# Product 2 of the gate and up projections by a second Strassen level, and a new order of a pair of tiles

## The chip, the cores and the metric

One NeuronCore of a Trainium2 chip runs the whole program. The metric is the device time of one execution in microseconds (us); lower is better. The engines run side by side, each with a queue of its own in order: TensorE (PE, matmuls), VectorE (DVE), ScalarE (ACT), GpSimdE (POOL) and SyncE (SP, which issues the DMAs).

## What is computed

One inference step of a hybrid decoder layer over 1048 tokens (16 meta tokens, 1024 of the prompt, 8 samples), in float32. Cut to what matters here:

```python
D_MODEL, D_FF = 1024, 2816

def swiglu(x, wg, wu, wd):
    return (jax.nn.silu(x @ wg) * (x @ wu)) @ wd

h = h + 0.5 * swiglu(rmsnorm(h, n1), w1g, w1u, w1d)      # FFN 1
...                                                      # two scans (HGRN2, Mamba-2) and projections
h = h + 0.5 * swiglu(rmsnorm(h, n2), w2g, w2u, w2d)      # FFN 2
```

The change is in the gate and up projections (`x @ wg`, `x @ wu`) of both FFNs.

## The kernel before

**Numbers.** A float32 factor is split into a high part (a cast to the reduced type float32r, on ScalarE) and a low part (the rest, a subtraction on VectorE). A product of two factors is then three matmuls: high-high, high-low, low-high (`mm3`, lines 163 to 165).

**Blocks.** Tokens stand in the free dimension in four quarters of Q columns (262 in FFN 1, which has 1048 tokens, and 258 in FFN 2, where 16 are dropped). The 22 tiles of 128 hidden columns are worked in 11 pairs, `i` = 0 to 10; the tiles of a pair are here called a and b. Gate and up of a tile are one 2 x 2 block product (two weight matrices by two halves of the 1024 inputs; two quarters of tokens), made by Strassen's scheme in its Winograd form: seven products named 1, 5, 6, 7, 2, 3, 4, of four k-tiles each, for each of the two halves c of the tokens. One product for one half is one step of 12 matmuls. `Blocks` makes the token operands, `Left` the weight operands: `load` (DMA on SP), `sum_` (VectorE, line 460), `hi` (ScalarE cast, line 464), `lo` (VectorE, line 468).

**The nested part.** In pairs 3 to 10 product 3 of the two tiles is not done outright: `Inner` treats product 3 of a and of b together as one more 2 x 2 product and does it by seven inner products of two k-tiles and Q columns (6 matmuls each, 42 for what would be 48). `Inner.operands` makes its token operands once in an FFN, `begin` its weight sums and splits, `product` its matmuls, and `post` adds the results to the partial sums x of the two tiles.

**PSUM.** Eight banks: two double banks (pool `acc`, both halves c of one outer product) and four single ones (pool `mis`, the inner products). A double bank is taken when the first matmul into it is issued and comes free when its last reader has run.

**Order.** In the FFNs the order of TensorE, VectorE, ScalarE and SP is written by hand. `Steps` is a list of matmul steps; `before(i, fn)` hangs work ahead of step i, and what is hung there is issued to the other engines' queues in that order, then the step's matmuls, then its `post`. So each engine's queue has a fixed order. A pair before: a's products 1, 6, 2, 5, 7, then b's 1, a's 4, b's 2, 6, 5, 7, inner 1 6 and 5 7, b's 4, inner 2 3 and 4. After product 4 of both, `post` multiplies by the norm factor (`times_r`, line 670), ScalarE applies SiLU, and VectorE multiplies gate by up (`product_`, line 717) into a hidden tile.

**After a pair.** `Hidden.jobs` makes four differences of hidden blocks (line 954), which the down projection's own Strassen products need, into extra tiles, and stores all seven blocks to DRAM (line 957). `down` follows pair 10: its loads, casts (line 979) and lows (line 983) of the first hidden operands, and those of its weights (lines 1040, 1045), begin some steps before the gate and up stage ends.

Fixed pools that matter: 6 weight tiles `ws` (high and low together), 8 raw weight tiles `r`, 9 temporaries `t`, 8 slots `s` and 30 slots `u`.

Of the kernel before, what the change touches and what calls it, by code (L numbers as in the profile page):

```python
# [17 lines left out]
P = 128  # L18
D = 1024
# [423 lines left out]
class Left:  # L443
# [12 lines left out]
    def sum_(self, p):  # L456
        x, y, op = {5: (7, 4, ALU.add), 6: (5, 1, ALU.subtract), 7: (1, 7, ALU.subtract), 3: (2, 6, ALU.subtract)}[p]
        if p not in self.raw:
            self.raw[p] = self.K.raw(self.n * P)
        self.K.nc.vector.tensor_tensor(self.raw[p], self.raw[x], self.raw[y], op)  # L460
# [68 lines left out]
ORDER6 = (1, 6, 2, 5, 7, 4), (1, 2, 6, 5, 7, 4)  # L529


class Inner:
# [4 lines left out]
    def __init__(self, K, ops, op=None):  # L537
        self.K, self.ops = K, ops
        self.op = {} if op is None else op
        self.raw, self.w, self.ps = {}, {}, {}  # L540
        self.then, self.out = {}, {}

    def next(self):
        return Inner(self.K, self.ops, self.op)

    def half(self, c, h):
        n = 2 * self.K.Q
        return tuple(x[:, h * n : h * n + n] for x in self.ops[c].op[3])

    def operands(self):  # L550
# [3 lines left out]
        t = K.slot("u", K.T)  # L554
        a, b, d = t[:, :n], t[:, n : 2 * n], K.slot("s", K.T)[:, :n]
# [23 lines left out]
    def begin(self, S, s0):  # L579

        K, nc = self.K, self.K.nc
        f, g = self.raw.pop(0), self.raw.pop(1)
        tmp = K.slot("u", K.T)
        s = tmp[:, :512]
        self.z, self.v = (tmp[:, 512 + i * K.Q : 512 + i * K.Q + K.Q] for i in range(2))

        def sums():
            nc.vector.tensor_add(s[:, :256], g[:, :256], g[:, 256:])
            nc.vector.tensor_sub(s[:, 256:], s[:, :256], f[:, :256])

        def sum7():
            nc.vector.tensor_sub(g[:, :256], f[:, :256], g[:, :256])

        def sum3():
            nc.vector.tensor_sub(f[:, 256:], f[:, 256:], s[:, 256:])

        def hi(i, src):
            self.w[i] = K.ws()
            nc.scalar.copy(self.w[i][:, : src.shape[1]], src)

        def lo(i, src):
            w = src.shape[1]
            nc.vector.tensor_sub(self.w[i][:, 512 : 512 + w], src, self.w[i][:, :w].bitcast(F32))

        for at, fn, *args in (
            (2, sums), (3, sum7), (5, hi, 0, f), (6, lo, 0, f), (6, sum3), (6, hi, 1, s), (7, lo, 1, s),
            (7, hi, 2, g), (8, lo, 2, g), (9, hi, 3, f[:, 256:]), (10, lo, 3, f[:, 256:]),
        ):
            S.before(s0 + at, lambda fn=fn, args=args: fn(*args))

    def step(self, S, *ps):

        def mm():
            for p in ps:
                self.product(p)
                self.post(p)

        S.add(mm)

    def product(self, p):  # L620
        K = self.K
        b = {2: 1, 3: 5, 4: 7}.get(p, p)
# [3 lines left out]
        i, o = {1: (0, 0), 2: (0, 256), 5: (1, 0), 6: (1, 256), 7: (2, 0), 4: (2, 256), 3: (3, 0)}[p]  # L626
# [6 lines left out]
    def post(self, p):  # L633
        nc = self.K.nc
        add = nc.vector.tensor_add
        z, v, x, y = self.z, self.v, self.out[0](), self.out[1]()
        ps = self.ps[{2: 1, 3: 5, 4: 7}.get(p, p)]
        if p == 1:
            nc.scalar.copy(z, ps)
        elif p == 6:  # L640
            add(v, ps, z)
            add(y, y, v[:, None, :].broadcast_to([P, 2, self.K.Q]))
            add(x[:, 1], x[:, 1], v)
        elif p == 5:
            add(y[:, 1], ps, y[:, 1])
        else:
            t = {7: y[:, 1], 2: x[:, 0], 3: x[:, 1], 4: y[:, 0]}[p]
            add(t, ps, t)


def pair(K, S, wg, wu, f, ops, spread, hid, late_r, first=None, inner=None):
# [21 lines left out]
    def post(p, cs, b):  # L673
# [11 lines left out]
        elif p == 7:  # L685
            nc.vector.tensor_add(temp("u1", cs), b, temp("x", cs))
            if inner:
                times_r("u1", 1, cs)
# [6 lines left out]
        elif inner:  # L695
            t = temp("v", cs)
            nc.vector.tensor_add(t, b, t)
            tm["u0"] = tm["v"]
            times_r("u0", 0, cs)
            product_(0, cs)  # L700
# [17 lines left out]

    if inner:
        i = f % 2  # L720
        left.plan(S, s0, 0, 2 * i, ORDER6[i], ((0, 2, 4, 6, 8, 12), (0, 4, 6, 8, 10, 14))[i])
        unit = Unit(K, left.w, [o.op for o in ops], 4, post)

        def both(*ps):
            for p in ps:
                for c in range(2):
                    unit.step(S, p, c, (0, 1))

        def keep():
            inner.raw[i] = left.raw[3]  # L730

        cs = slice(0, 2)

        def gate():
            tm["g1"] = tm["x"]
            silu(1, cs)

        S.before(s0, keep)
        inner.then[i] = (gate, lambda: product_(1, cs))
        inner.out[i] = lambda: temp("x", cs)  # L740
        if i == 0:
            both(1, 6, 2, 5, 7)
            inner.last = lambda: both(4)
            return
        S.before(s0 + 3, lambda: inner.begin(S, s0 + 2))
        both(1)
        inner.last()
        both(2, 6, 5, 7)
        inner.step(S, 1, 6)
        inner.step(S, 5, 7)  # L750
        both(4)
        inner.step(S, 2, 3)
        inner.step(S, 4)
        e = len(S.steps)
        for at, fn in ((0, inner.then[0][0]), (2, inner.then[1][0]), (3, inner.then[0][1]), (5, inner.then[1][1])):
            S.before(e + at, fn)
        return
# [63 lines left out]
def plain_tiles(K, S, wg, wu, x, ops, spread, columns1, columns, hid):  # L821
# [107 lines left out]
class Hidden:  # L929
# [1599 lines left out]
```

## Time and profile before

| | us |
|---|---|
| median of 3 runs | 1920.61 |
| lowest and highest | 1920.38, 1921.33 |
| the profiled execution, its own time | 1921.17 |
| its span in the trace | 1919.4 |
| mean granted TensorE clock | 0.998 |

The profile is of one execution. Its rows give, for a group or a single instruction: start and duration in us, the engine, the line of the code, the operation, the tile written and the tiles read, and the shape (partitions x elements); in brackets the idle time before it and what ended that. FFN 1's gate and up stage lies at about 50 to 475 us, FFN 2's at about 1250 to 1680 us.

### The profile page before, as it was taken

To read this page: it belongs to the slowest core of one execution; us is meant where nothing else is said; L and a number is where in the kernel's file an instruction comes from. 1 tells how busy PE (TensorE), PEld (TensorE's weight loads), DVE (VectorE), ACT (ScalarE), POOL (GpSimd) and SP (SyncE) were. 2 spreads that over 40 slices of the span, in tenths; PEclk is the share of its full clock that TensorE was granted. 3 is DMA by queue.
4 is the path that set the end of the run, shared out by engine and by line. 5 is a ranking of instruction groups with operands and counts; after the bars stand their busy time and mean duration, and the time that the engine had idled before them with its cause. 6 is when DMAs were issued, how large, how long until landed. Compare 5 with 4: busy or idle time off the path is not lost.

```text
span 1919.4 us, 41103 instructions
## 1 busy us (share of the span) xinstructions
PE 1902.5 (99%) x16588; PEld 1870.2 (97%) x16588; DVE 1527.1 (80%) x2791; ACT 844.2 (44%) x1646; POOL 84.9 (4%) x159
## 2 busy tenths in 40 slices
PE   9999999999999999999999999999999999999998
PEld 8999999999999999999999999999999999999997
DVE  7888888888788877576776667998888888878965
ACT  7632332323543644466554565742323323453353
POOL 3000000000000410000000002200000000000000
PEclk9999999999999999999999999999999999999999
DMA  8152333325977551132453154322323333597852
GB/s 241 35 151 87 103 101 96 111 90 160 299 227 254 162 164 51 50 102 69 134 139 113 54 172 149 99 85 84 111 89 102 104 95 111 163 261 232 278 180 79
DMA packets 324647, 258.48 MB, mean 135 GB/s; under 512 B 17825, under 2 KB 299681, under 8 KB 324449
## 3 DMA queue, kind: packets, MB, share of 16 engines
q1 hardware_dynamic: 324213, 255.80, 44.1%
q8 instruction: 131, 2.15, 0.5%
q14 instruction: 59, 0.48, 0.1%
q0 software_dynamic: 224, 0.04, 0.0%
q10 hardware_dynamic: 20, 0.01, 0.0%
HBM read 191.84 MB, written 64.01 MB: 133 GB/s over the span
## 4 chain that ended last, share of the span: by engine, by line
PE 91%; DVE 5%; ACT 1%; DMA 1%; issue 1%; SPq 0%; DVEq 0%; POOL 0%; POOLq 0%; ACTq 0%
PE acc L163 27%; PE acc L165 27%; PE acc L164 26%; PE mis L163 1%; PE mis L165 1%; PE mis L164 1%; PE mis L1988 1%; DMA r<-in_w_ffn_up_dram 1%; PE mis L1614 0%; PE mis L2060 0%; DVE ws L468 0%; DVE u L983 0%; PE mis L1605 0%; DVE t L303 0%; DMA u<-hd 0%
## 5 line engine op out<-in xcount | busy, mean ns | idle before, releaser
L163 PE MATMUL acc<-u,ws 128*128 128x258 f32 (+3 forms) x4210 | 1228.6, 292 | 2.2 <-ACT t L918 1.0
L165 PE MATMUL acc<-u,ws 128*128 128x258 f32 (+3 forms) x4210 | 1217.4, 289 | 0.1
L164 PE MATMUL acc<-u,ws 128*128 128x258 f32 (+3 forms) x4210 | 1216.4, 289 | 0.3 <-DVE u L306 0.2
L163 PEld LDWEIGHTS acc<-u,ws 128*128 128x128 f32 x4210 | 794.0, 189 | 9.4 <-issue 4.6
L164 PEld LDWEIGHTS acc<-u,ws 128*128 128x128 f32 x4210 | 797.5, 189 | 2.3 <-DVE u L306 0.7
L165 PEld LDWEIGHTS acc<-u,ws 128*128 128x128 f32 x4210 | 792.8, 188 | 0.6 <-DVE ws L158 0.3
L468 DVE TENSOR_TENSOR ws<-r,ws 128x512 fp32r<-128x512 f32 x268 | 184.7, 690 | 69.8 <-ACT ws L464 69.6
L464 ACT CAST ws<-r 128x512 fp32r<-128x512 f32 x268 | 155.4, 615 | 13.0 <-ACT ws L464 8.4
L460 DVE TENSOR_TENSOR r<-r,r 128x512 f32<-128x512 f32 x168 | 116.0, 692 | 1.9 <-DMA r<-in_w_ffn_up_dram 0.5
L682 ACT ACTIVATE t<-t 128x516 f32<-128x516 f32 (+1 forms) x41 | 26.2, 639 | 207.0 <-DVE t L670 207.0
L711 ACT ACTIVATE t<-t 128x516 f32<-128x516 f32 (+1 forms) x43 | 27.5, 639 | 191.7 <-DVE t L670 191.7
L983 DVE TENSOR_TENSOR u<-u,u 128x1048 fp32r<-128x1048 f32 (+3 forms) x84 | 97.0, 1157 | 5.1 <-ACT u L979 4.7
L232 POOL TENSOR_TENSOR t<-t,t 128x262 f32<-128x262 f32 (+1 forms) x56 | 54.7, 987 | 806.8 <-ACT t L231 803.6
L670 DVE TENSOR_TENSOR t<-t,u 128x516 f32<-128x516 f32 (+1 forms) x127 | 87.7, 697 | 2.8
L158 DVE TENSOR_TENSOR ws<-r,ws 128x512 fp32r<-128x512 f32 x88 | 60.9, 703 | 33.9 <-ACT ws L157 33.8
L1040 ACT CAST ws<-u 128x512 fp32r<-128x512 f32 (+1 forms) x72 | 42.1, 585 | 102.9 <-DVE u L1035 100.9
L979 ACT CAST u<-u 128x1048 fp32r<-128x1048 f32 (+3 forms) x84 | 82.8, 988 | 0.0
L1040 ACT CAST ws<-r 128x512 fp32r<-128x512 f32 (+1 forms) x84 | 47.9, 582 | 70.3 <-DVE r L1035 31.5
L1069 DVE SCALAR_TENSOR_TENSOR s<-acc,s 128x524 f32<-128x524 f32 (+3 forms) x86 | 53.7, 648 | 29.4 <-PE acc L165 29.1
L1045 DVE TENSOR_TENSOR ws<-r,ws 128x512 fp32r<-128x512 f32 (+1 forms) x84 | 57.5, 694 | 22.9 <-ACT ws L1040 22.9
L157 ACT CAST ws<-r 128x512 fp32r<-128x512 f32 x88 | 53.9, 618 | 34.9 <-PE acc L165 27.4
L1045 DVE TENSOR_TENSOR ws<-u,ws 128x512 fp32r<-128x512 f32 (+1 forms) x72 | 46.8, 650 | 26.5 <-ACT ws L1040 26.5
(465 smaller groups left out, 2341.4 us busy)
## 6 DMA issues: line engine op xcount, KB each, us to landing
r<-in_w_ffn_down_dram SPq DMA_DIRECT2D x128, 256.0 KB
hd<-s SPq DMA_DIRECT2D x93, 258.0 KB
r<-in_w_ffn_gate_dram SPq DMA_DIRECT2D x88, 256.0 KB
r<-in_w_ffn_up_dram SPq DMA_DIRECT2D x88, 256.0 KB
hd<-s SPq DMA_DIRECT2D x77, 262.0 KB
u<-hd SPq DMA_DIRECT2D x36, 516.0 KB
u<-hd SPq DMA_DIRECT2D x28, 524.0 KB
r<-in_w_in_dram SPq DMA_DIRECT2D x56, 256.0 KB
```

The source lines that it names most:

```text
L158: self.nc.vector.tensor_sub(lo, src, hi.bitcast(F32))
L163: mm(ps, whi, xhi, start=first, stop=False, skip_group_check=more)
L164: mm(ps, whi, xlo, start=False, stop=False, skip_group_check=more)
L165: mm(ps, wlo, xhi, start=False, stop=last, skip_group_check=more)
L460: self.K.nc.vector.tensor_tensor(self.raw[p], self.raw[x], self.raw[y], op)
L464: self.K.nc.scalar.copy(self.w[p][:, : self.n * P], self.raw[p])
L468: self.K.nc.vector.tensor_sub(t[:, 512 : 512 + w], self.raw[p], t[:, :w].bitcast(F32))
L670: nc.vector.tensor_mul(t, t if src is None else src, spread.lanes(i, cs))
L979: K.nc.scalar.copy(hi, lo.bitcast(F32))
L983: K.nc.vector.tensor_sub(lo, lo.bitcast(F32), hi.bitcast(F32))
L1040: nc.scalar.copy(w[p, j, g][:, : n * P], src)
L1045: nc.vector.tensor_sub(t[:, 512 : 512 + n * P], box[0], t[:, : n * P].bitcast(F32))
```

## The change

Product 2 of a pair (pairs 3 to 10) now also goes through an `Inner`: there are two sets, N (product 2) and M (product 3). Token operands for N are made once in an FFN, like M's, in pairs 2 and 3. A pair has its own function, `nested_pair`, with a step list and a plan of all work as text.

- Outer products 1, 6, 7, 4 of a tile add up in one double bank, without being cleared between; product 5 has the other. Before the next product is added, ScalarE copies the partial sum (after 1: `z`; after 6: `v`, after 7: `w`, each half c by itself). VectorE then has one add after 6, one add and one `times_r` after 7, one `times_r` after 4.
- The inner products 1, 6, 7, 4 do the same in one single bank, with 5 and 3 in a second and 2 in a third. ScalarE copies after 1, 6 and 7.
- Order: a's 1, M 1 5, a's 5, M 6 2, a's 6, M 7 3, a's 7, M 4, a's 4, and the same for b with N. M belongs to the pair before: its weights are split at the end of its own pair, and its sums, gates, products and stores run on into the next pair. Pair 3 has no M; pair 10 does its own M (called L) at its end.
- Weight loads are issued three steps before the first cast. The differences of hidden blocks are made in place. In `down`, the last two loads of the first operands and their casts come later (steps -2, +1, +2 instead of -9, -7, -4, -2), and the first weights' casts and lows up to four steps later.
- Shared temporaries in the pairs that are not nested, and later stores in pair 0.

```diff
-ORDER6 = (1, 6, 2, 5, 7, 4), (1, 2, 6, 5, 7, 4)
...
     def product(self, p):
         K = self.K
-        b = {2: 1, 3: 5, 4: 7}.get(p, p)
+        b = {6: 1, 7: 1, 4: 1, 3: 5}.get(p, p)
         new = b == p
...
     def post(self, p):
...
-        if p == 1:
+        if p in (1, 7):
             nc.scalar.copy(z, ps)
         elif p == 6:
-            add(v, ps, z)
-            add(y, y, v[:, None, :].broadcast_to([P, 2, self.K.Q]))
-            add(x[:, 1], x[:, 1], v)
+            nc.scalar.copy(v, ps)
         elif p == 5:
-            add(y[:, 1], ps, y[:, 1])
+            add(y[:, 1], ps)
+        elif p == 2:
+            add(x[:, 0], ps, z)
+        elif p == 3:
+            add(x[:, 1], ps, v)
+            add(y[:, 1], z)
         else:
-            t = {7: y[:, 1], 2: x[:, 0], 3: x[:, 1], 4: y[:, 0]}[p]
-            add(t, ps, t)
+            add(y[:, 0], ps)
...
+STEPS2 = "a1 M15 a5 M62 a6 M73 a7 M4 a4 b1 N15 b5 N62 b6 N73 b7 N4 b4"
+STEPS3 = "a1 M15 a5 M62 a6 M73 a7 M4 a4 b1 N15 b5 N62 b6 N73 L15 b7 N4 L62 b4 L73 L4"
+
+PLAN2 = {
+    -8: "da1 da7 da4", -5: "ha1", -4: "la1 sa5", -3: "da2", -2: "ha5", -1: "la5 sa7 sa6", 1: "ha6", 2: "la6 sa3", 4: "ha7", 5: "la7 db1 db7 db4",
+    7: "ha4", 8: "la4 db2", 9: "hb1", 10: "lb1 sb5", 11: "N+ Nh0", 12: "hb5 Nl0 Nh1", 13: "lb5 Nl1 sb7 sb6", 14: "N-", 15: "hb6", 16: "lb6 sb3 Nh2",
+    17: "Nl2", 18: "hb7", 19: "lb7", 20: "Nh3", 21: "Nl3 hb4", 22: "lb4", 24: "ga0", 26: "pa0", 27: "gb0", 28: "S1", 30: "pb0", 32: "S2",
+}
+PLAN_M = {25: "M+ Mh0", 26: "Ml0 Mh1", 27: "Ml1", 28: "M-", 30: "Mh2", 31: "Ml2", 34: "Mh3", 35: "Ml3",
+    38: "ga1", 40: "pa1", 41: "gb1", 42: "D5", 43: "pb1", 44: "S5", 45: "S3 D7", 47: "S7", 48: "D6", 50: "S6 D4", 52: "S4"}
+PLAN_L = {18: "M+ Mh0", 19: "Ml0 Mh1", 20: "Ml1", 21: "M-", 24: "Mh2", 25: "Ml2", 26: "Mh3", 27: "Ml3",
+    31: "ga1", 32: "gb1", 33: "pa1", 34: "pb1", 35: "D5", 36: "S3 D7", 37: "S5", 38: "S7", 39: "D6", 41: "S6 D4", 43: "S4"}
...
+    def step(x, p, c):
+        b = 5 if p == 5 else 1
+        if (x, b) not in banks:
+            banks[x, b] = K.psum2()[:, :, : K.Q]
+        ps = banks[x, b]
+        product(K, ps[:, c], lefts[x].w[p], ops[c].op[p], 4, p in (1, 5), True, p not in (1, 5))
+        if p in (6, 7):
+            nc.scalar.copy(temp(x, "v" if p == 6 else "w")[:, c], ps[:, c])
+        if not c:
+            return
+        if p == 1:
+            nc.scalar.copy(temp(x, "z"), ps)
+        elif p == 6:
+            nc.vector.tensor_add(temp(x, "x"), banks[x, 5], temp(x, "v"))
+        elif p == 7:
+            nc.vector.tensor_add(temp(x, "w"), banks[x, 5], temp(x, "w"))
+            times_r(x, "u1")
+        elif p == 4:
+            times_r(x, "u0", ps)
...
-            at = [b + k for k in (-14, -11, -11, -9, -9, -7)], [b + k for k in (-8, -7, -6, -5, -4, -2)]
+            at = [b + k for k in (-14, -11, -11, -9, -2, -2)], [b + k for k in (-8, -7, -6, -5, 1, 2)]
...
-                    pieces(p, j, g, b + 6 * j + 2 * g, None)
+                    pieces(p, j, g, b + 6 * j + 2 * g, None, (4, 3, 2, 1)[3 * j + g] if a == 0 and 3 * j + g < 4 else 0)
```

How the plan reads: the number is the step of the pair ahead of which the work is issued (negative: in the pair before; 28 and above: in the next). In a step list a letter and a digit of a or b are two steps (c = 0, 1); M15 is one step of two inner products. In the plan `d`, `s`, `h`, `l` are load, sum, high part and low part of a weight; `N+`, `N-` the inner weight sums (two narrow VectorE operations each), `Nh0`, `Nl0` its splits; `ga0` the norm factor on gate half 0 of tile a (VectorE) with SiLU (ScalarE), `pa0` gate times up; `D5` a difference, `S5` a store.

More of the change, by code (lines that the diff above doesn't have):

```diff
@@ L577, in operands @@
         ], [lambda: cast(4, b), lambda: low(4, b)]
[L579 to L618, printed above, removed]
+    def begin(self, f, g, tmp, out):
+        self.f, self.g, self.out = f, g, out
+        self.s = tmp[:, :512]
+        self.z, self.v = (tmp[:, 512 + i * self.K.Q : 512 + i * self.K.Q + self.K.Q] for i in range(2))
+        self.w, self.ps = {}, {}
+    def sums(self):
+        nc, s, f, g = self.K.nc, self.s, self.f, self.g
+        nc.vector.tensor_add(s[:, :256], g[:, :256], g[:, 256:])
+        nc.vector.tensor_sub(s[:, 256:], s[:, :256], f[:, :256])
@@ L694, in post @@
             times_r("u1", 1, cs)
[L695 to L700, printed above, removed]
         else:
@@ L717, in product_ @@
         nc.vector.tensor_mul(halves(hid[0][:, n * 2 * K.Q : n * 2 * K.Q + 2 * K.Q])[:, cs], temp(f"g{n}", cs), temp(f"u{n}", cs))
[L719 to L757, printed above, removed]
     if not first:
@@ L1128, in ffn, with operands, make @@
         hidden = Hidden(K)
-        inner = Inner(K, ops)
+        inners = {"N": Inner(K, ops, 2), "M": Inner(K, ops, 3)}
+        def operands(name, at, step, late):
+            def make():
+                tiles = [K.t(2 * K.Q) for n in range(3)] if name == "N" else wide()
+                made, last = inners[name].operands(tiles)
+                for n, fn in enumerate(made):
+                    S.before(at + step * n // 2, fn)
+                for n, fn in enumerate(last):
+                    S.before(late + n, fn)
+            S.before(at - 1, make)
@@ L1130, in ffn, with wide @@
+        def wide():
+            n, t = 2 * K.Q, K.slot("u", K.T)
+            return t[:, :n], t[:, n : 2 * n], K.slot("s", K.T)[:, :n]
         for i in range(NF // 2):
-            hid, e = [], []
-            rec = inner.next() if i >= 3 else None
+            s0 = len(S.steps)
+            if i >= 3:
+                nested_pair(K, S, wgv, wuv, i, ops, spread, inners, hidden, i == NF // 2 - 1)
+                continue
             if i == 1:
-                def operands(s0=len(S.steps) + 18):
-                    made, late = inner.operands()
-                    for n, fn in enumerate(made):
-                        S.before(s0 + 5 * n // 2, fn)
-                    for n, fn in enumerate(late):
-                        S.before(s0 + 46 + 3 * n, fn)
-                S.before(len(S.steps) + 17, operands)
@@ L1143, in ffn @@
-            for f in (2 * i, 2 * i + 1):
-                hid.append([])
-                if plain and i == 0:
-                    continue
-                pair(K, S, wgv, wuv, f, ops, spread, hid[-1], late_r, first if f == 0 else None, rec)
-                e.append(len(S.steps))
-            ats = None
+                operands("M", s0 + 18, 5, s0 + 54)
+                operands("N", s0 + 40, 4, s0 + 70)
+            hid = [[], []]
             if plain and i == 0:
                 plain(S, wgv, wuv, hid)
-                e = [len(S.steps) + 15] * 2
-                ats = {p: e[0] + 5 + n for n, p in enumerate((1, 3, 2, 5, 6, 7, 4))}
-            elif i == 0:
+                e = len(S.steps) + 20
+                hidden.jobs(S, i, hid, (e, e + 1, e + 2), ((e + 2, e + 5), (e + 3, e + 6), (e + 4, e + 8), (e + 6, e + 10)))
+                continue
@@ L1155, in ffn @@
+            e = []
+            for f in (2 * i, 2 * i + 1):
+                pair(K, S, wgv, wuv, f, ops, spread, hid[f % 2], late_r, first if f == 0 else None)
+                e.append(len(S.steps))
+            if i == 0:
                 e = late_r + 6, max(late_r + 7, e[1])
-            hidden.jobs(S, i, hid, *e, rec, ats)
+            hidden.jobs(S, i, hid, (e[0] + 2, e[1] + 1, e[1] + 2), ((e[0] + 4, e[0] + 8), (e[1] + 2, e[1] + 5), (e[1] + 4, e[1] + 8), (e[1] + 6, e[1] + 10)))
         h = []
```

157 lines of the change are left out of this document (111 added, 46 removed).

## The prediction

> **What bounds the kernel now.** I read the page first, then stretches of it, then single rows of the gate and up stages.
>
> ```profile
> span 1919.4 us, 41103 instructions
> PE 1902.5 (99%) x16588; PEld 1870.2 (97%) x16588; DVE 1527.1 (80%) x2791; ACT 844.2 (44%) x1646; POOL 84.9 (4%) x159
> PE 91%; DVE 5%; ACT 1%; DMA 1%; issue 1%; SPq 0%; DVEq 0%; POOL 0%; POOLq 0%; ACTq 0%
> ```
>
> TensorE bounds the whole; VectorE comes second, at 80%. The next rows are the steady nested pairs of the two FFNs and the last stretch of each gate/up stage (columns: length, busy us and count of PE, PEld, DVE, ACT, POOL, granted clock, DMA share, GB/s).
>
> ```profile
> 220.00:440.00 220.00, 220.00 (x1803) 220.00 (x1802) 190.94 (x330) 66.60 (x126) 0.00 (x0) 1.00 0.32 97
> 1460.00:1660.00 200.00, 200.00 (x1665) 199.62 (x1664) 173.82 (x302) 61.40 (x116) 0.00 (x0) 1.00 0.34 102
> 460.00:480.00 20.00, 19.38 (x159) 19.17 (x158) 19.33 (x30) 10.70 (x17) 0.00 (x0) 1.00 0.66 197
> 1660.00:1680.00 20.00, 19.32 (x162) 19.11 (x161) 18.48 (x31) 11.47 (x18) 0.00 (x0) 1.00 0.82 248
> ```
>
> A matmul takes 220/1803 = 0.122 us in FFN 1 (262 columns) and 200/1665 = 0.120 us in FFN 2 (258), at full clock, and TensorE hardly waits. VectorE is busy 87% there: a pair is 330 matmuls or 39.6 us (FFN 2), so VectorE has some 5 us to spare in it. What the change asks of VectorE, and when, decides.
>
> **What is saved.** A pair loses the 48 matmuls of product 2 and gains 42 of its inner products: 6 fewer, in 8 pairs of each FFN. 48 x 0.120 + 48 x 0.122 = **11.6 us**, all on the path.
>
> [...] The rows above say 120 and 122, and I take them.
>
> **What VectorE gets.** Two lows (product 2's), four post operations and a wide inner add go; the second inner product brings three wide lows and, narrow, four sums, a low and seven adds. 48 wide and 12 narrow operations a pair become 44 and 24. What an operation costs in the queue is the distance between starts:
>
> ```profile
> 1501.01 0.70 DVE L697 TENSOR_TENSOR t<-acc,t 128x516 f32<-128x516 f32 x1 [1.04 <-PE acc L165]
> 1501.74 0.70 DVE L670 TENSOR_TENSOR t<-t,u 128x516 f32<-128x516 f32 x1
> 1502.47 0.69 DVE L717 TENSOR_TENSOR s<-t,t 128x516 f32<-128x516 f32 x1
> 1503.09 0.42 DVE L588 TENSOR_TENSOR u<-r 128x256 f32<-128x256 f32 x1
> 1503.54 0.42 DVE L589 TENSOR_TENSOR u<-u,r 128x256 f32<-128x256 f32 x1
> 1503.88 0.68 DVE L468 TENSOR_TENSOR ws<-r,ws 128x512 fp32r<-128x512 f32 x1
> 1504.48 0.42 DVE L592 TENSOR_TENSOR r<-r,r 128x256 f32<-128x256 f32 x1
> 1511.46 1.41 DVE L460 TENSOR_TENSOR r<-r,r 128x512 f32<-128x512 f32 x2
> ```
>
> Wide: 0.60; when it uses the one before it, 0.73 (1501.01 to 1501.74; of two sums of L460 that touch one tile the second comes 0.72 later). Narrow: 0.34, or 0.45. The new pair: 26.6 + 8.2 = 34.8 us, some 0.8 more for those that use the one before, so 35.6 of 324 x 0.120 = 38.9 us: 92% instead of 87%. On average it fits, but the new order bunches it.
>
> **The bank that is late.** Two double banks serve the outer products. Tile a now keeps one from product 1 to product 4; it is free when VectorE has multiplied it (`times_r` u0), and product 5 of tile b takes it, 67 matmuls after the last of a's product 7 (6 of M4, 24 of a4, 24 of b1, 12 of N15, and itself). TensorE does wait for such a read now:
>
> ```profile
> 1530.96 0.69 DVE L670 TENSOR_TENSOR t<-acc,u 128x516 f32<-128x516 f32 x1
> ...
> 1531.62 0.28 PE L165 MATMUL acc<-u,ws 128*128 128x258 f32 x1
> 1531.79 0.36 PE L163 MATMUL acc<-u,ws 128*128 128x258 f32 x1
> 1531.99 0.28 PE L164 MATMUL acc<-u,ws 128*128 128x258 f32 x1
> ```
>
> The read ends at 1531.65 and product 7 starts 0.14 later, with its second matmul stretched to 0.20: about 0.2 us between a read's end and full pace. Product 5 there had taken the other bank, which was freed first, so banks go in the order they come free, and the new order gives b1 the one that product 7 frees and b5 the late one. ScalarE's prices:
>
> ```profile
> 1512.93 0.28 PE L165 MATMUL mis<-u,ws 128*128 128x258 f32 x1
> 1513.25 0.38 ACT L639 COPY u<-mis 128x258 f32<-128x258 f32 x1 [3.15 <-PE mis L165]
> 1513.52 0.62 ACT L464 CAST ws<-r 128x512 fp32r<-128x512 f32 x1
> 1664.34 0.64 ACT L682 ACTIVATE t<-t 128x516 f32<-128x516 f32 x1 [5.78 <-DVE t L670]
> 1664.88 0.60 ACT L464 CAST ws<-r 128x512 fp32r<-128x512 f32 x1
> 1665.38 0.62 ACT L599 CAST ws<-r 128x512 fp32r<-128x512 f32 x1
> 1667.47 1.06 ACT L979 CAST u<-u 128x1032 fp32r<-128x1032 f32 x1
> 1668.49 0.62 ACT L1040 CAST ws<-r 128x512 fp32r<-128x512 f32 x1
> ```
>
> A copy of a half bank starts 0.04 after the last matmul ends and takes 0.38 (0.27 to the next), a SiLU 0.54, a cast 0.52, a wide cast 1.0.
>
> Now VectorE's queue in FFN 2 by these distances, from 0 = end of a's product 7. Start times: add w 0.46 (behind ScalarE's copy), u1 1.18, N's sums 1.79 and 2.24, M4's add 2.58, product a1 2.92, N low 3.53, gate b1 4.13, low b5 4.74, N low 5.34, sums b7 and b6 5.94 and 6.66, u0 at last 7.26, done 7.95. TensorE would start b5 at -0.28 + 67 x 0.120 = 7.77 and starts at about 8.15: **0.38 waited**. The queue goes on, without a gap, to N's second add at 13.6, then D6 and a low, idles till b6's copy (15.97), and then has D4, a low, three adds, gate a0, a low and a sum (0.6 x 6 + 1.15 = 4.8) where b7's add should start at 20.29: it starts at 20.75, 0.45 late. The same twelve operations follow on b's side, so the next tile's product 5 waits 0.38 + 0.45 = **0.82**. After that half comes a gap of 2 us, which takes the lateness away again: 1.2 a pair. In FFN 1 a matmul is 0.002 longer (67 of them 0.13) and the wide operations a little: 0.26 and 0.66. From the pair after the first nested one to the last, with the lateness not yet there at its beginning: 8.0 us (FFN 2) and 6.0 us (FFN 1). Below, it is bounded by 0, where three of the twelve (1.9 us) are done earlier; above by what a low waits for its cast now:
>
> ```profile
> L468 DVE TENSOR_TENSOR ws<-r,ws 128x512 fp32r<-128x512 f32 x268 | 184.7, 690 | 69.8 <-ACT ws L464 69.6
> ```
>
> 69.6/268 = 0.26 each, three lows in front of each of 28 reads: 22 us more. In the count each cast is done before its low is reached, so I take none of it.
>
> **Start of the nesting.** The second operand set costs VectorE 12 wide operations, 7.3 us, in pairs 2 and 3, and pair 3 has no M steps, so its products 1, 5, 6, 7, 4 come without cover. Pair 2's u0 stands behind a gate, an M low, a weight low and two sums: 2.8 us after its product's end. 2.8 + 0.69 + 0.2 against 24 matmuls less 0.16 (2.7): 0.9 waited by a5. a6 needs a low that stands seven operations on (4.5 us): 1.6 more. With 0.2 for b5, 2.8 and 2.5 us. Bounds 0 (VectorE ahead by then) and 6.
>
> **The last pair.** There M runs as L in the same pair, with its sums and lows in steps 18 to 21 (2.7 us more, of which 0.8 us was idle: b6's add starts 1.9 after b6), and down's operands come in: four wide casts in ScalarE's queue in steps 24 to 27, each ahead of a partial-sum copy that VectorE or TensorE needs. Counted from b6's end: VectorE reaches gate a0 at 5.2, done 5.9; SiLU, M cast, wide cast, copy, wide cast, copy 3.65: 9.7; VectorE's add w, u1, product, wide low (1.14), add, gate 4.0: 13.6; ScalarE's SiLU, wide cast and copy 1.9, and 0.2 to TensorE: 15.9 to 16.2. L's product 7 could start at 10.6. So 5.5 us, 0.4 for product 4 (copy of 7), and 2.7 for down's third operand group, whose lows stand behind six late operations: 8.7 and 8.3 us. Nearest to this is now's last pair:
>
> ```profile
> 1674.48 0.42 DVE L603 TENSOR_TENSOR ws<-r,ws 128x256 fp32r<-128x256 f32 x1
> 1676.22 1.23 DVE L983 TENSOR_TENSOR u<-u,u 128x1032 fp32r<-128x1032 f32 x1
> 1677.37 0.69 DVE L1045 TENSOR_TENSOR ws<-r,ws 128x512 fp32r<-128x512 f32 x1
> 1677.97 0.42 DVE L645 TENSOR_TENSOR t<-mis,t 128x258 f32<-128x258 f32 x1
> 1678.44 0.39 PE L163 MATMUL mis<-u,ws 128*128 128x258 f32 x1 [0.68 <-DVE t L645]
> ```
>
> There the inner product 3 waits for an add that stands behind down's wide lows; the same adding-up of the queue for the kernel before gives 0.95 us at this place, as the trace has it, and none in the pairs ahead. Bounds: 1 each (as now) and 12.
>
> **Hidden or without price.** Fewer stores' temporaries, differences in place (D6 waits for a store that was issued 3 steps ahead) and jobs of pair 0: 0. Loads of a tile's weights are issued 3 steps (4.3 us) before their cast instead of 6, behind the stores on SP.
>
> ```profile
> 5.11 6.92 DMA r<-in_w_ffn_up_dram
> 96.75 5.41 DMA r<-in_w_ffn_up_dram
> ```
>
> Issued at 12.5 in the count above, they land at 17.9 with 5.4, and the cast's low is due at 19.5: 0; with 6.9 about 0.4 a half pair, 11 us in all at most. ScalarE's thirteen more half copies (0.27) and two more casts a pair, 4.6 us, fit beside its 31% now: 0 but where counted.
>
> **The sum.** Waits 8.0 + 6.0 + 2.8 + 2.5 + 8.7 + 8.3 = 36.3; now's own at the same places go (0.95, 0.9 in FFN 1, and 0.13 a pair in FFN 2 as shown, 1.0): 2.9. 36.3 - 2.9 - 11.6 = **+21.8 us**. The profiled execution took 1921.17 (span 1919.4), 0.6 above the median of the runs, 1920.61; on that, **1942 us**.
>
> **Rivals.** (1) *Faster.* VectorE reads the bank in time: if u0 ran ahead of the lows and sums queued before it (3.7 us of them), all steady waits and most of the tail's would go, leaving some 5: 5 - 2.9 - 11.6, 1911 us, and everything between 1909 and 1916 with less cover. It decides when all waits stay under 14.5 us. For it: VectorE's 92%. Against: VectorE's rows stand now in the order in which the code issues them. (2) *No change.* Only the steady waits come, start and tail as now: 14.0 - 1.0 - 11.6, 1922 us. Against it: four wide casts ahead of copies. (3) *Worse.* Weights land late (up to 11), and each weight tile of the last pair waits for one of six slots: 1958 or more. For it: in steps 18 to 21 of the last pair seven weight tiles live.
>
> [...] The rows above start 0.08 before the end of the last, so I give it 0.02.
>
> **How the numbers follow.** A measurement of this kernel tells about 0.2% (3.8 us) from no change. Forecast (1931 to 1957): 0.66; between no change and it (1925 to 1931): 0.08; no change: 0.06; faster: 0.12; above 1957, with rival 4: 0.08. So slower 0.82, same 0.06, faster 0.12. The range 1917 to 1957 leaves out 0.08 above and some 0.1 below.
>
> **What will show it.** 96 fewer matmuls, VectorE near 90% in steady pairs; product 5 of each tile starting just after a `times_r` from the bank, TensorE gaps of 0.3 to 0.9 us twice a pair; 2.5 us of gaps in the first nested pair and 8 in the last, the longest at L's product 7, released by ScalarE. Steady gaps under 0.2, or a tail like now's, would make the prediction wrong.

## The result, and the profile after

The changed kernel takes 1988.72 us (median of 4 runs, 1987.13 to 1989.70), the kernel before 1920.68 on the same chip: a ratio of 1.035, 95% interval 1.0335 to 1.0371. It is slower, by 68 us, where 21.8 were forecast. The profiled execution of the changed kernel took 1987.13 us, 1.6 below its median.

The page, its head and the two groups that matter (columns: count, busy us, mean ns of one, idle us of the engine before them and what ended most of it):

```profile
span 1985.3 us, 41267 instructions
...
PE 1922.2 (97%) x16492; PEld 1869.6 (94%) x16492; DVE 1562.1 (79%) x2943; ACT 942.2 (47%) x1894; POOL 84.5 (4%) x159
...
L163 PE MATMUL acc<-u,ws 128*128 128x258 f32 (+4 forms) x3954 | 1167.2, 295 | 44.4 <-ACT t L776 38.3
...
L776 ACT COPY t<-acc 128x262 f32<-128x262 f32 (+1 forms) x128 | 48.2, 376 | 143.1 <-PE acc L165 143.1
```

The 96 matmuls are gone (16588 to 16492). But TensorE now idles 38.3 us in front of the first matmul of a group (L163 is the first line of `mm3`) until a copy of line 776 has ended. That line is `nc.scalar.copy(temp(x, "v" if p == 6 else "w")[:, c], ps[:, c])` in `nested_pair`: the half copies of the partial sums after products 6 and 7. What TensorE waited for, in order of cost (what waited, for what; us in total, times, longest; rows of this form below are of the same view):

```profile
PE acc L163 <- ACT t L776: 38.3, 68, 3.1
PE acc L164 <- DVE u L1025: 2.2, 2, 1.1
PE mis L163 <- ACT u L627: 1.9, 2, 1.6
```

Product 6 or 7, its first half done, in a steady pair of FFN 2:

```profile
1508.78 0.28 PE L165 MATMUL acc<-u,ws 128*128 128x258 f32 x1
...
1509.09 0.38 ACT L776 COPY t<-acc 128x258 f32<-128x258 f32 x1 [1.48 <-PE acc L165]
...
1509.52 0.39 PE L163 MATMUL acc<-u,ws 128*128 128x258 f32 x1 [0.47 <-ACT t L776]
...
1509.75 0.29 PE L164 MATMUL acc<-u,ws 128*128 128x258 f32 x1
```

The last matmul of half 0 starts at 1508.78 and ends at 1509.06. The copy of half 0 runs at once, from 1509.09 to 1509.47. The next matmul, the first of half 1, starts at 1509.52, though it writes the other bank: 0.74 from start to start instead of 0.12, and 0.23 to the one after it, so 0.73 us are lost. This happens at products 6 and 7 of both tiles in 16 nested pairs: 64 x 0.73 = 46.7 us.

The stretches of the steady pairs, shown before for the old kernel, give the same (same columns):

```profile
220.00:440.00 220.00, 209.78 (x1654) 203.39 (x1653) 185.50 (x350) 92.86 (x195) 0.00 (x0) 1.00 0.32 95
1460.00:1660.00 200.00, 190.13 (x1520) 184.27 (x1519) 168.49 (x320) 85.47 (x180) 0.00 (x0) 1.00 0.34 100
```

200 us hold 1520 matmuls instead of 1665. A pair of 324 loses 324 x (200/1520 - 0.120) = 3.75 us: four times 0.73, 0.34 and 0.38 at the two products 5, and 0.1 in smaller pieces. The same sum is made below for each experiment.

At each product 5 TensorE goes on just after a `times_r` (line 766) has read the late bank, as here in FFN 2:

```profile
1502.29 0.69 DVE L766 TENSOR_TENSOR t<-acc,u 128x516 f32<-128x516 f32 x1
...
1502.67 0.29 PE L165 MATMUL mis<-s,ws 128*128 128x258 f32 x1
...
1503.03 0.39 PE L163 MATMUL acc<-u,ws 128*128 128x258 f32 x1
```

For the account of whole kernels, the excess over 0.120 us (FFN 2) or 0.122 (FFN 1) between the starts of consecutive matmuls is added up, wherever it is more than 0.02, over each FFN's gate/up stage and the first products of down (100 to 520 us and 1250 to 1760 us). It is 40.7 and 40.5 us in the changed kernel, 1.8 and 2.9 in the one before. 81.2 - 4.7 - 11.6 = 64.9 of the 68 us. (1.7 more lie at 928 us, in a stage that the change does not touch; see the last section.)

### The profile page after: what moved, and what is told of

Read it like the earlier page. It is cut to its first block, busy times and chain, and to the rows that moved or that the text cites. A ratio compares the mean times of both kernels' runs of the same rounds, so it can differ in the third digit from the quotient of the medians.

```text
span 1985.3 us, 41267 instructions
## 1 busy us (share of the span) xinstructions
PE 1922.2 (97%) x16492; PEld 1869.6 (94%) x16492; DVE 1562.1 (79%) x2943; ACT 942.2 (47%) x1894; POOL 84.5 (4%) x159
## 5 line engine op out<-in xcount | busy, mean ns | idle before, releaser
L163 PE MATMUL acc<-u,ws 128*128 128x258 f32 (+4 forms) x3954 | 1167.2, 295 | 44.4 <-ACT t L776 38.3
L164 PE MATMUL acc<-u,ws 128*128 128x258 f32 (+4 forms) x3954 | 1146.5, 290 | 2.5 <-DVE u L1025 2.2
L165 PE MATMUL acc<-u,ws 128*128 128x258 f32 (+4 forms) x3954 | 1146.0, 290 | 0.9 <-DVE ws L470 0.8
L163 PEld LDWEIGHTS acc<-u,ws 128*128 128x128 f32 x3954 | 747.0, 189 | 71.0 <-ACT t L776 52.4
L164 PEld LDWEIGHTS acc<-u,ws 128*128 128x128 f32 x3954 | 750.0, 190 | 5.1 <-DVE u L1025 3.1
L165 PEld LDWEIGHTS acc<-u,ws 128*128 128x128 f32 x3954 | 746.3, 189 | 1.6 <-DVE ws L470 1.3
L466 ACT CAST ws<-r 128x512 fp32r<-128x512 f32 x236 | 143.0, 620 | 69.8 <-DVE r L462 66.1
L470 DVE TENSOR_TENSOR ws<-r,ws 128x512 fp32r<-128x512 f32 x236 | 162.0, 687 | 9.8 <-ACT ws L466 9.7
L776 ACT COPY t<-acc 128x262 f32<-128x262 f32 (+1 forms) x128 | 48.2, 376 | 143.1 <-PE acc L165 143.1
L158 DVE TENSOR_TENSOR ws<-r,ws 128x512 fp32r<-128x512 f32 x88 | 61.0, 703 | 36.0 <-ACT ws L157 36.0
L163 PE MATMUL mis<-u,ws 128*128 128x258 f32 (+1 forms) x294 | 84.0, 286 | 0.0
L165 PE MATMUL mis<-u,ws 128*128 128x258 f32 (+1 forms) x294 | 83.6, 284 | 0.0
L164 PE MATMUL mis<-u,ws 128*128 128x258 f32 (+1 forms) x294 | 83.5, 284 | 0.0
L782 DVE TENSOR_TENSOR t<-acc,t 128x524 f32<-128x524 f32 (+1 forms) x32 | 22.4, 700 | 68.2 <-ACT t L776 68.1
```

Of the source, the lines that this page charges most:

```text
L158: self.nc.vector.tensor_sub(lo, src, hi.bitcast(F32))
L163: mm(ps, whi, xhi, start=first, stop=False, skip_group_check=more)
L164: mm(ps, whi, xlo, start=False, stop=False, skip_group_check=more)
L165: mm(ps, wlo, xhi, start=False, stop=last, skip_group_check=more)
L466: self.K.nc.scalar.copy(self.w[p][:, : self.n * P], self.raw[p])
L470: self.K.nc.vector.tensor_sub(t[:, 512 : 512 + w], self.raw[p], t[:, :w].bitcast(F32))
```

## The experiments

By the guard of a tile is meant here whatever holds a write to a tile back until its earlier readers have run. Theory A: the wait is the guard of a tile. Both halves of the outer product stand in one tile of two banks; a write to one half waits for the last reader of the tile, although that reader is in the other bank. Rivals: the copies cost ScalarE too much time (C); VectorE's queue sets the pace and the waits only show it (B); TensorE cannot write beside ScalarE's read of a neighbouring bank (E).

| run | time, us | to before, 95% | pair's waits, FFN 2 | stage waits, FFN 1 + 2 |
|---|---|---|---|---|
| changed kernel | 1988.7 | 1.0335 to 1.0371 | 3.75 | 40.7 + 40.5 |
| one copy | 1952.0 | 1.0146 to 1.0176 | 1.67 | 23.1 + 23.8 |
| two copies, late | 1953.7 | 1.0160 to 1.0194 | 1.85 | 24.0 + 25.2 |
| one copy, u0 first | 1945.8 | 1.0114 to 1.0145 | 1.14 | 19.4 + 20.8 |
| u0 first alone | 1981.4 | 1.0301 to 1.0331 | 3.33 | 36.7 + 38.7 |
| single-bank tiles | 1938.3 | 1.0068 to 1.0098 | 0.37 | 16.5 + 16.4 |
| single-bank tiles, u0 first | 1931.9 | 1.0038 to 1.0072 | 0.18 | 13.6 + 13.9 |

The runs of the kernel before beside them had medians of 1921.13 and 1921.54 us. In each row before's 1921, plus the two stage waits, less 4.7 and 11.6, comes within 4 us of the measured time.

**One copy.** Both halves are copied together, after the second half's matmuls.

```diff
-        if p in (6, 7):
-            nc.scalar.copy(temp(x, "v" if p == 6 else "w")[:, c], ps[:, c])
         if not c:
             return
+        if p in (6, 7):
+            nc.scalar.copy(temp(x, "v" if p == 6 else "w"), ps)
```

> Products 6 and 7 of a nested pair copy both halves of their partial sum in one ScalarE copy, after the second half's matmuls. Theory A (the second half's matmuls wait for the first half's copy, 0.73 us at each of 64 places): 64 x 0.73 = 46.7 us go and 1942 comes, or up to 1952 if VectorE, which caught up in these waits, becomes late at product 5. Rival B (VectorE's queue sets the pace, and the waits only show it): the time comes back at product 5 and at the last pair, 1979 to 1990. Rival C (a copy takes ScalarE time, thirteen more a pair): one copy of 0.6 for two of 0.38 saves 32 x 0.16 = 5 us, 1983.

1951.97 us: 36.8 of the 46.7 us go. B and C forecast 1979 or more; A's upper end is met. What came back is not where the forecast had it; the waits of TensorE:

```profile
PE acc L163 <- ACT t L778: 11.5, 18, 1.7
PE mis L163 <- ACT u L627: 6.0, 2, 3.0
```

Of the 18 waits for the copy (now line 778), 16 are at product 4, which must not start before the copy of product 7; only the inner product 4, six matmuls or 0.72 us, lies between. The other two are at product 7 of tile a in pair 3, where no inner product lies between. On tile b a SiLU stands ahead of the copy (timeline of the same run):

```profile
1491.37 0.64 ACT L813 ACTIVATE t<-t 128x516 f32<-128x516 f32 x1 [2.64 <-DVE t L766]
...
1491.91 0.57 ACT L778 COPY t<-acc 128x516 f32<-128x516 f32 x1
...
1492.53 0.39 PE L163 MATMUL acc<-u,ws 128*128 128x258 f32 x1 [0.46 <-ACT t L778]
```

The copy of the whole tile takes 0.57 instead of 0.38 and starts 0.54 late: product 4 waits 0.73 on tile b, 0.23 on tile a. With 0.40 and 0.37 at the products 5 that is the pair's 1.7.

**Two copies, late.** The same two half copies as in the changed kernel, both after the second half.

```diff
-        if p in (6, 7):
-            nc.scalar.copy(temp(x, "v" if p == 6 else "w")[:, c], ps[:, c])
         if not c:
             return
+        if p in (6, 7):
+            for k in range(2):
+                nc.scalar.copy(temp(x, "v" if p == 6 else "w")[:, k], ps[:, k])
```

> The same two half copies as in the changed kernel, but both issued after the second half's matmuls. Theory A: like the single copy, 1942 to 1953 (the sum's add can begin 0.1 to 0.2 later). Rival B: 1979 to 1990. Rival C (ScalarE's time): all of the copies are still there, so 1985 to 1989.

1953.73 us, within 2 us of the single copy. ScalarE has as many copies as in the changed kernel, so its time (C) is not the price; their place is.

**u0 first, with one copy and alone.** The reads that free the late bank are issued ahead of what stood before them.

```diff
-    -1: "la5 sa7 sa6",
+    0: "la5 sa7 sa6",
-    13: "lb5 Nl1 sb7 sb6", 14: "N-",
+    14: "Nl1 lb5 sb7 sb6 N-",
-    27: "gb0", 28: "S1",       27: "Ml1", 28: "M-",       41: "gb1", 42: "D5",
+    28: "gb0 S1",              28: "Ml1 M-",              42: "gb1 D5",
```

> One copy, and on VectorE each tile's times_r of u0 (the read that frees the late bank) is issued ahead of the low, the two sums, the inner low, the gate that stood in front of it. Theory A with the late bank (0.38 and 0.82 a pair as forecast): the product 5 waits go below 0.1, 8 to 14 us less than with the one copy alone, 1930 to 1938. Rival D (VectorE at 92% is the limit, so any order is late somewhere): within 3 us of the one copy alone, the waits coming back at products 6, 7 or 4 of the next tile, on a low.

> The changed kernel with only the early times_r of u0: the copies by halves stay. Theory A with the late bank: the product 5 waits of 0.35 twice a pair go, 9 to 10 us, 1978 to 1981; the 64 waits of 0.73 stay. Rival D: within 3 us of the changed kernel.

1945.84 with one copy (6.1 us less than without u0 first, 8 to 14 forecast) and 1981.38 alone (7.3 less, 9 to 10 forecast): under both forecasts of the late bank, and outside the 3 us of D. The time forecast with one copy, 1930 to 1938, is missed by 8 us. The pair's waits fall by 0.53 (1.67 to 1.14) and 0.42 (3.75 to 3.33). The products 5 no longer wait; up to 0.1 a tile remains at an inner product. At the start of the nesting, product 5 of pair 3 now waits 1.5 us for a low that stands behind u0.

**Single-bank tiles.** The half copies stay where they are; each half is a tile of its own.

```diff
-        if (x, b) not in banks:
-            banks[x, b] = K.psum2()[:, :, : K.Q]
-        ps = banks[x, b]
+        if (x, b, c) not in banks:
+            banks[x, b, c] = K.psum()[:, : K.Q]
+        ps = banks[x, b, c]
...
+        for k in range(2):      # the adds after 6 and 7 and the u0 product, one per half
...
+                if i == 3:
+                    S.before(s0, lambda: K.banks(1))    # four single banks; two doubles again at down
```

> The changed kernel with its half copies where they are, but each half of a double bank is a tile of its own (four single banks instead of two doubles); reads over both halves become two reads of a half (VectorE 3 more operations a tile, about 0.09 us each). Theory A (the wait is the guard of the two-bank tile, not the hardware): the 64 waits of 0.73 go with every copy still in its place, 1942 to 1953. Rival E (TensorE cannot write one bank while ScalarE reads its neighbour): they stay, 1985 to 1992.

1938.25 us, 50.5 below the changed kernel, 13.7 below the single copy and 4 below A's range: with the shorter copies product 4 no longer waits either, and product 5 waits once a pair, 0.36. The copies run and TensorE does not stop (timeline):

```profile
1478.17 0.28 PE L164 MATMUL acc<-u,ws 128*128 128x258 f32 x1
1478.24 0.38 ACT L776 COPY t<-acc 128x258 f32<-128x258 f32 x1 [1.49 <-PE acc L165]
1478.28 0.28 PE L165 MATMUL acc<-u,ws 128*128 128x258 f32 x1
1478.40 0.28 PE L163 MATMUL acc<-u,ws 128*128 128x258 f32 x1
1478.53 0.28 PE L164 MATMUL acc<-u,ws 128*128 128x258 f32 x1
```

During the copy of half 0 (1478.24 to 1478.62) matmuls of half 1 start every 0.12 us. Line 776 made 192 copies in this run, and TensorE waited for 2 of them, 1.3 us together, in the last pairs; in the changed kernel it waited 68 times. E is out, and A is shown: the copies after products 6 and 7 are the same and stand in the same place. Besides the tile's extent, only the copy after product 1 and three reads by VectorE a tile are split by halves, which adds operations and takes none away. So the guard over two banks waited for more than these rows need, 0.73 us each time.

The steady stretch of four kernels, one copy, two late copies, single-bank tiles, single-bank tiles with u0 first:

```profile
1460.00:1660.00 200.00, 196.56 (x1598) 192.88 (x1598) 176.48 (x335) 85.71 (x168) 0.00 (x0) 1.00 0.34 99
```
```profile
1460.00:1660.00 200.00, 195.84 (x1591) 192.00 (x1590) 175.70 (x333) 85.72 (x188) 0.00 (x0) 1.00 0.34 99
```
```profile
1460.00:1660.00 200.00, 199.38 (x1651) 198.47 (x1651) 184.67 (x377) 92.23 (x204) 0.00 (x0) 1.00 0.35 101
```
```profile
1460.00:1660.00 200.00, 200.00 (x1659) 199.31 (x1658) 186.63 (x380) 91.17 (x203) 0.00 (x0) 1.00 0.34 100
```

In the last row TensorE is full with VectorE busy 93% (six more operations a pair): the new pair does fit beside VectorE when nothing else is in its way.

**Single-bank tiles with u0 first** (both edits).

> Tiles of one bank and u0 first. If both causes add up: 8 to 14 us below the tiles alone, and no wait for a copy at the start of the nesting either (2 x 0.94 in each FFN), 1928 to 1938. Rival D (VectorE's load is the limit): within 4 us of the tiles alone.

1931.89 us, 6.4 less than the tiles alone (8 to 14 forecast, within 4 by D): both causes add up, the second a little short of its forecast. What is left is the start and the last pair; the waits of TensorE:

```profile
PE mis L163 <- ACT u L625: 8.7, 2, 4.4
PE acc L163 <- DVE t L687: 3.6, 2, 1.8
```

The second row is the change from two double banks to four single ones: product 1 of pair 3 waits till pair 2's last bank is read. The first is L's product 4 in the last pair, behind the copy of product 7.

**Cover of twelve.** Inner products in the order 1, 6 2, 7 5, 4 3, on the single copy with u0 first (the gates ga0, gb0, ga1, gb1 and their products come one to four steps later).

```diff
-b1 N15 b5 N62 b6 N73 b7 N4 b4
+b1 N1 b5 N62 b6 N75 b7 N43 b4      (and M likewise)
```

> On top of the one copy with u0 first: the inner products are put in the order 1, then 6 2, then 7 5, then 4 3, so that twelve inner matmuls (1.44 us) instead of six (0.72) lie between product 7 and product 4, and the gates come after product 4. With one copy alone the wait of product 4 for product 7's copy was 0.73 on tile b (a SiLU stood ahead of the copy) and 0.23 on tile a. Theory A: both go, 7 x 0.96 in each FFN, 13 us: 1931 to 1936. Rival (ScalarE or VectorE has no room, so the wait moves): 1942 to 1946.

1981.59 us, 36 slower. (In this kernel FFN 2 does not compute the same; its time alone is read.) In the steady pairs product 4 no longer waits, but the gates moved behind it stand, with u0, ahead of the next tile's lows; the waits of TensorE:

```profile
PE acc L165 <- DVE ws L470: 26.4, 30, 1.2
PE mis L163 <- ACT u L625: 11.5, 29, 0.4
```

The rival had the kind, the wait moves, but not the size (1942 to 1946): the third matmul of a group waits for a low of its weights, 30 times.

**The last pair.** Five runs tried to shorten the 8 to 9 us that each FFN still loses there.

| run (on single-bank tiles, u0 first) | time, us | to before, 95% | stage waits |
|---|---|---|---|
| last pair's product 3 outright | 1932.4 | 1.0041 to 1.0071 | 13.3 + 14.2 |
| tail order | 1930.0 | 1.0032 to 1.0057 | 12.8 + 11.3 |
| tail order, nested from pair 4 | 1931.8 | 1.0042 to 1.0069 | 11.1 + 11.5 |
| tail order, lows behind | 1928.8 | 1.0031 to 1.0059 | 12.6 + 12.2 |
| tail order, inner products spread | 1953.1 | 1.0153 to 1.0181 | 24.2 + 24.8 |

The intervals of the first four overlap each other and that of the run they build on (1.0038 to 1.0072), so by their times alone they are not told apart; what they tell is where TensorE waits.

```diff
 last pair's product 3 outright
-STEPS3 = "... a7 M4 a4 b1 N15 b5 N62 b6 N73 L15 b7 N4 L62 b4 L73 L4"
+STEPS3 = "... a7 M4 a4 a3 b1 N15 b5 N62 b6 N73 b7 N4 b4 b3"
 tail order
-    24: "ga0", 26: "pa0", 28: "gb0 S1", 30: "pb0", 32: "S2"        casts of down's groups 0, 1: b - 8 ... b - 5
+    25: "ga0", 27: "pa0", 28: "S1", 32: "gb0", 33: "pb0", 35: "S2"                              b - 7 ... b - 4
-operands("N", s0 + 40, 4, s0 + 70)
+operands("N", s0 + 44, 4, s0 + 72)
 nested from pair 4
-if i >= 3:                 operands("M", s0 + 18, 5, s0 + 54)    operands("N", s0 + 40, 4, s0 + 70)
+if i >= 4:                 operands("M", s0 + 18, 6, s0 + 82)    operands("N", s0 + 62, 5, s0 + 98)
 lows behind
-casts b - 7, - 6, - 5, - 4, lows one step after each             operands("M", ..., s0 + 54)
+casts b - 7, - 6, - 3, - 1, lows at b - 6, - 4, - 2, b           operands("M", ..., s0 + 60)
 inner products spread
-nested_pair(..., i == NF // 2 - 1)
+nested_pair(..., i >= 4)          (M's deferred steps run in pair 4 alone)     operands("M", ..., s0 + 60)
```

> As the run before it, and the last pair of each FFN computes product 3 outright (48 matmuls) instead of by the inner products of L (42): 0.7 us more TensorE a FFN, but VectorE loses four lows, four sums and seven adds there and gains two lows and four half adds, and ScalarE's wide casts no longer stand between inner products. If the tail's waits (8 us a FFN with the one copy) are due to that queue: 8 to 13 us below the run before it. Rival (down's operand casts alone hold the tail): 0 to 3 us below, or 1 above.

Its product 3 multiplies a right-hand operand of which M's fourth operand has overwritten a part, so its time alone is read. No gain: L's wait is gone, and one of 5.0 us stands at down's first product, which takes double banks again and so waits for the last single one to be read (L784, behind down's lows):

```profile
PE acc L163 <- DVE t L784: 10.1, 2, 5.0
```

> Single-bank tiles and u0 first, and in the last pair tile b's gate g0 and its product come after L's last inner product instead of ahead of it, a's gate and down's four wide operand casts one step later, behind the partial-sum copies; the second inner operand set is built 4 steps later. If the tail's wait (4.6 us at L's product 4, for a copy of L's product 7 that stands behind tile b's SiLU and three casts, some 1.8 at product 4 and L's product 6 behind wide casts, and the half clock that follows, 1.6) is the order of ScalarE's queue: it falls from 8.3 and 8.9 to 2 to 4 a FFN, the start's 3.5 to 2.5: 1916 to 1923. Rival (VectorE's wide lows hold the tail whatever ScalarE's order): within 4 us of 1932.

1929.95: 1.9 less, not the 9 to 16 forecast, and within the 4 of the rival. The waits of TensorE got shorter and more:

```profile
PE mis L163 <- ACT u L625: 4.4, 4, 1.9
PE acc L163 <- DVE t L788: 3.6, 2, 2.1
PE acc L163 <- DVE t L687: 3.6, 2, 1.8
```

> As the run before it, with the nesting from pair 4 instead of pair 3: pair 3 computes products 2 and 3 outright, 12 matmuls more in each FFN (1.44 us), and the second operand set is spread over one pair more. If the start's wait (3.5 us) is VectorE's lateness from these operands, it goes: 1 to 2 us faster than the run before it. Rival (it is the change from double banks to single ones, which waits for all of them): 2 to 3 us slower.

1931.79, 1.8 slower than the tail order alone. Spreading the operand set saves nothing at the first nested product:

```profile
PE acc L163 <- DVE t L687: 3.6, 2, 1.8
```

The last two operations of M's set still stood two steps ahead of it; the next run, which issues them behind it, halves this wait. The rest is put down to the read of the last double bank itself (L687), which no run here takes away.

> As e12, and in the last pair VectorE's wide lows of down's operands and the last two wide casts are issued two to four steps later, behind the adds of L's products and u0 of tile b; the last two operations of the first inner operand set come 6 steps later. e12 still waits 2.13 us at L's product 7 or 4 (a copy behind VectorE's wide low), 1.93 at down's first product (u0 behind three lows), loses 1.7 of every 3.4 us that follow at half clock (6.8 us in each FFN), and 2.0 at the start. If it is the order of VectorE's queue: the tail goes from 6.6 to 1 to 3 a FFN without a stretch at half clock, the start to 1, 1916 to 1922. Rival (VectorE has more to do in the last pair than fits before down, in any order): the wait moves to down's first operands, 1927 to 1931.

1928.77: the rival again. TensorE's waits for copies and for u0 halve, the start's falls from 3.6 to 1.8, and the delayed lows of down's operands are late in their turn:

```profile
PE acc L164 <- DVE u L1028: 6.7, 4, 2.2
PE mis L163 <- ACT u L625: 2.6, 4, 1.0
PE acc L163 <- DVE t L788: 1.9, 2, 1.0
PE acc L163 <- DVE t L687: 1.8, 2, 0.9
```

> From pair 4 on every nested pair adds up both inner products in itself (M in tile b's half as in the last pair, 15 after N's 7 3, then 62 and 73 between and behind), so that the deferred M and the pair's own one meet in pair 4, which has no operand casts of down, and not in the last pair. If the tail's waits (6.6 to 8.7 us a FFN in the three runs before) are VectorE's and ScalarE's work that piles up there (some 6 us of L's sums, lows and adds on top of four wide lows of 1.15): the last pair comes to 1 to 3 us, pair 4 gets 1 to 3, and no stretch at half clock follows: 1914 to 1922. Rival (down's operands alone hold the tail, or tile b's half is too full in every pair): 1926 to 1940.

1953.08, slower by 24. With L in every pair from 4 on, the next pair's lows are late 12 times (the row below); that the gates pile up ahead of them on ScalarE and VectorE at each pair's end is read from the order of issue and was not tested. The waits of TensorE and the steady stretch (2.6 us a pair):

```profile
PE acc L165 <- DVE ws L470: 7.9, 12, 0.7
```
```profile
1460.00:1660.00 200.00, 192.33 (x1563) 188.54 (x1563) 176.91 (x357) 87.23 (x196) 0.00 (x0) 1.00 0.33 98
```

And the last pair, now without the deferred M, still loses 7.1 us in FFN 1 and 5.8 in FFN 2, against 7.3 and 7.5 with the tail order. So its wait is neither the order of the two queues alone nor the deferred M alone; every one of these orders only moved it. What would take it away stays open: no run here removed down's operand casts from that place.

The best version, 1928.8 us, is still 0.3 to 0.6% slower than the kernel before.

## Why the prediction was wrong, step by step

**The step that failed: "ScalarE's thirteen more half copies (0.27) and two more casts a pair, 4.6 us, fit beside its 31% now: 0 but where counted."** The time on ScalarE does fit (the two late copies show it). What was left out is who waits for each copy. The order of issue had it in plain sight: product, half 0; copy of half 0; product, half 1, into the same tile. The duration was quoted (a copy starts 0.04 after the last matmul and takes 0.38), and so was the 0.2 us from the end of a read to full pace: 0.04 + 0.38 + 0.2 is 0.62 of the 0.73. 64 of them are 46.7 us, and 1988.7 less 46.7 is 1942.0, the forecast to the microsecond. That agreement is partly luck, as the other terms show.

- *Saved matmuls, 11.6 us*: right. 96 fewer; a matmul still takes 0.120 and 0.122.
- *VectorE at 92%*: right as work. With one copy it is busy 176.48 of 200 us, 35.8 us of a pair of 40.6; counted were 35.6.
- *The late bank, 1.2 a pair (0.38 and 0.82)*: right in place and kind (each product 5 starts behind a `times_r` that has read the bank, and u0 first removes it), twice too big in the second term: 0.37 and 0.40 with one copy, 0.36 once a pair with single-bank tiles. The 0.45 of lateness carried from one tile to the next did not come, not even with single-bank tiles, where no wait at product 4 gives VectorE time to catch up; why stays open.
- *Product 4 behind product 7's copy, not counted*: with half copies it is covered (0.62 against 0.72); with one copy it costs 0.96 a pair, some 13 us in 14 pairs. The late bank came some 3 us short of its 14.0, the starts and last pairs together within 1 of their 22.3: so it is this term that made 1952 of 1942.
- *Start of the nesting, 2.8 and 2.5*: 1.25 and 1.15 beside the half copies. Products 5 and 6 of tile a wait, as forecast, for about half as long.
- *Last pair, 8.7 and 8.3*: 9.8 (FFN 2) and 10.4 (FFN 1), with the half copies. The kind was right, ScalarE's wide casts ahead of copies, but the longest wait came earlier, at tile b's product 7, whose second half waits for the first half's copy behind a SiLU and two casts (ScalarE's timeline in FFN 1; TensorE goes on at 492.43, 3.4 after the matmul in front):

```profile
489.99 0.64 ACT L813 ACTIVATE t<-t 128x524 f32<-128x524 f32 x1 [0.52 <-DVE t L766]
490.54 0.60 ACT L595 CAST ws<-r 128x512 fp32r<-128x512 f32 x1
491.05 1.06 ACT L1021 CAST u<-u 128x1048 fp32r<-128x1048 f32 x1
492.01 0.37 ACT L776 COPY t<-acc 128x262 f32<-128x262 f32 x1
...
```

L's product 7 waited 1.85 there (0.57 in FFN 2), not 5.5, since that delay had already been paid. With one copy the longest wait does stand where it was forecast, at L's product 7 behind a SiLU, a wide cast and a copy: 3.0 us (the row of L627 under that run), with a stretch at half clock behind it (granted clock 0.50 from 484.6 to 488.0 and from 1706.6 to 1710.0).

- *Rivals.* The faster one had the right lever (u0 ahead of lows and sums is worth 6 to 7 us) and the wrong size: 11.6 us saved never covered the start and the last pair. Rival 3 gave a time on the right side with the wrong cause: no load of weights is among TensorE's waits in the two stages. Rival 4, given 0.02, has no run on its side either: in the changed kernel an operation of VectorE that does not use the one in front still starts 0.08 us before that one has ended (a low of 0.68 at 1499.76, the next low at 1500.36), and a pair fits into 39 us with VectorE 93% busy (single-bank tiles, u0 first).

## What to carry to other kernels

Price a new copy or read twice: its time on its own engine, and the next writer of whatever tile it reads. A tile that spans two banks was one thing to its guard, so a reader put between two halves stopped the second half for its whole duration (0.73 us lost here with a copy of 0.38); give the halves tiles of their own, or read both after the second. A place where several queues are full (here the last pair before down) was not mended by order: each new order there moved the wait.

## What the runs showed of the hardware

In the last pair TensorE ran at half clock (granted clock 0.50) for a while after some of its gaps, but not after all (stretches of the changed kernel; the granted clock is the third number from the right):

```profile
490.00:492.00 2.00, 0.00 (x0) 0.00 (x0) 0.69 (x1) 2.00 (x3) 0.00 (x0) 1.00 1.11 344
...
494.00:496.00 2.00, 2.00 (x19) 2.00 (x18) 1.36 (x3) 1.65 (x3) 0.00 (x0) 1.00 0.01 4
...
512.00:514.00 2.00, 2.00 (x10) 2.00 (x10) 2.00 (x4) 0.00 (x0) 0.00 (x0) 0.50 0.63 212
...
1734.00:1736.00 2.00, 2.00 (x11) 2.00 (x11) 1.43 (x3) 1.63 (x3) 0.00 (x0) 0.50 0.01 2
```

In the changed kernel such a stretch lasts 3.4 us (511.5 to 514.9, 1733.5 to 1736.9), a matmul takes 0.22 instead of 0.12, and 1.5 to 1.7 us are lost. In FFN 2 it begins 1.3 us after the wait of 3.1 us at product 7. In FFN 1 the same wait (489.3 to 492.4) leaves the clock at 1.00, and the stretch begins later, in the second of two waits at down's first product (1.05 and 1.48 from start to start). The kernel before has none in these stages; its wait there is 0.68 us. Outside the change, the changed kernel has one more from 927.9 to 931.3, and three other runs have one that starts at 900.7 (nested from pair 4), 902.7 (single-bank tiles) and 905.1 us (one copy, u0 first). In the run with the tail order the stretch lasts twice as long, about 6.8 us, with TensorE partly idle in it:

```profile
1682.00:1688.00 6.00, 4.49 (x21) 4.19 (x21) 5.97 (x13) 0.88 (x2) 0.00 (x0) 0.50 0.85 262
```

In the changed kernel these three stretches last 3.413 us each and begin whole multiples of that apart (at 511.5, 927.9 and 1733.5: 122 and 236 steps). The granted clock by 2 us shows the same in eight other runs (one copy, one copy with u0 first, single-bank tiles, single-bank tiles with u0 first, nested from pair 4, tail order, lows behind, inner products spread): 3.4 or 6.8 us long, and 125 to 358 whole steps apart.

How long TensorE idled within one such step goes with what followed better than how long one wait is. The wait of 3.1 us in FFN 2 left 2.1 us of idling in the step ahead of the stretch (1730.05 to 1733.46: busy 1.30 of 3.41); in FFN 1 a step ended inside the wait, with 1.7 us on one side and 1.4 on the other (busy 1.73 and 1.99 of 3.41), and full clock followed both. It does not decide alone: the step ahead of the stretch in FFN 1 (508.08 to 511.49) has 1.65 us of idling, less than the 1.7 that full clock followed, and the one ahead of 927.9 has none. What starts a stretch is not shown further. In FFN 2 of the run with the tail order TensorE idled 1.9 us between 1678 and 1682 (busy 1.86 and 0.27 of 2.00), after 8 us without a gap, and the clock was halved from 1681.9 on.

So in the changed kernel a wait of 3.1 us cost 3.3 in FFN 1 and, with the 1.5 lost at half clock behind it, 4.8 in FFN 2, and the forecast of the last pair had no term for that.
